# Up-projection of one decoder layer: attention's Strassen units with five doubled products in place of seven single ones

## The chip, the cores and the metric

The kernel runs on one NeuronCore of a Trainium2 chip. The metric is the device time of one execution in microseconds; the median of the runs counts. PE is the matrix engine, PEld its weight loads, DVE the vector engine, ACT the scalar engine, POOL the GpSimd engine, SP the engine that only issues DMAs here. PSUM is the memory that matmuls write to; one of its banks holds 512 float32 for each of the 128 partitions.

## What is computed

One layer of a decoder over 512 tokens of width 2048 in float32. The part that matters here is the merge of the two branches and what stands around it:

```python
merged = jax.nn.sigmoid(g_a) * (y_a @ w_up_a[i]) + jax.nn.sigmoid(g_b) * (y_b @ w_up_b[i])
x = x + merged @ w_o[i]
```

`y_a` (gated spatial mixing) and `y_b` (stick-breaking attention) are 512 x 1024, both `w_up` are 1024 x 2048, and the gates `g_a`, `g_b` are 512 x 2048. Ahead of it stands the combined input projection, behind it the output projection `w_o`, a SwiGLU layer and a gate with per-layer embeddings.

## The kernel before

**Precision.** Each float32 operand is kept as a high part (`hi`, rounded by a copy on ACT) and a low part (`lo`, the rest, by a subtraction on DVE). A product is hi x hi + hi x lo + lo x hi; the first factor is the stationary one (weights), the second the moving one (activations).

**Units.** A unit is a 256 x 256 block of weights against 256 x 512 of activations, as a 2 x 2 matter of blocks. A plain unit ("P") does eight block products (`mm3` with 512 columns in pairs of blocks). A Strassen unit ("S") does seven products of 256 columns, with sums of blocks prepared ahead. `pair` works off all units that make one 256-wide stripe of the output (the index `j`, eight stripes in a stage): it takes the next weights, usually for two units at a time, and calls `Pair.add`. I call such a call with two units a pass. `Pair.add` runs over the seven products (L691) and, within each, over the two units of the pass.

**Single and doubled products.** A single product (L713 to L716) is `mm3`: three matmuls of 256 columns, wh x hi (L297), wh x lo (L298), wl x hi (L299), and products share banks: `a` and `q` take two products each, `z` one, `y` two, so four banks for a stripe. A doubled product (L695 to L705) is two matmuls at L703: wh against hi and lo side by side (512 columns), and wl against hi (256 columns) added into the left half. It fills a bank by itself, and the two halves have to be added afterwards. With five doubled products a stripe has five such banks and the bank `y`, six in all.

**Banks.** `bank()` hands out tiles of the pool `psm`, which has six banks; `small_bank()` has the other two, `psa`, for other use. A tile can only be written when the readers of the tile that had the bank before are through.

**Adding up.** In the last pass of a stripe, a generator puts the seven products together on ACT and DVE, one step behind each product: `mix` (L719) for single products, two ACT copies of 512 columns (L726) and six additions on DVE (L729); `mix_doubled` (L749) for doubled ones, with four ACT copies of 256 columns (L759) and, with five doubled, ten additions on DVE (L762).

**The stage of the up-projection** is the loop from L1383. For each stripe `j` there are: the pair for branch a (`"PPPP"`, two banks, 512-column matmuls), the pair for branch b (`"PPPP"` for `j` = 0, since `until` is 1 there, `"SSSS"` for `j` = 1 to 7), and for `j` = 1 to 5 a small projection `ple_pair` (two banks). Ahead of each pair the gate's stripe is loaded from DRAM (`gsp`, L1385, issued by SP at L526) into the lowest free place of the arena `wholes`. Three ticks later `gate` multiplies it by the row of norms (`scaled`, DVE, L1255) and takes the sigmoid (ACT, L1390). Then the pair's result is multiplied in: a's straight out of its two banks (DVE, L1399, two halves), b's out of the mixed tile (L1396). Last, a's stripe is added to b's (L1403), a's place in the arena is given back, and two ticks later the sum is stored (`mix`, L1377). The next stage, `w_o`, loads these stripes as its activations (`ms`) and splits them (ACT L287, DVE L288).

**Weights.** SP loads them, POOL adds a third block in flight (L371), DVE makes two more sums (L383), ACT the high parts (L367), DVE the low parts (L364). There are three slots of split weights, so those of about two passes stand ready ahead.

**Order.** Each engine works off its instructions in one order, which the framework fixes when the program is built; PE waits at the first matmul whose operand or bank is not ready. In the rows below, b's stripes begin where PE's rows change from 512 to 256 columns.

Of the kernel before, what the change touches and what calls it, by code (L numbers as in the profile page):

```python
# [71 lines left out]
def hybrid_layer(  # L72
# [44 lines left out]
    class Arena:  # L117
# [28 lines left out]
        def give(self, block):  # L146
            self.turns += 1
            self.given[block.start // P : -(-(block.start + block.n) // P)] = self.turns
            holes = sorted(self.holes + [(block.start, block.n)])
            self.holes = holes[:1]  # L150
            for s, n in holes[1:]:
                if sum(self.holes[-1]) == s:
                    self.holes[-1] = (self.holes[-1][0], self.holes[-1][1] + n)
                else:
                    self.holes.append((s, n))
# [48 lines left out]
    def after(n, fn):  # L204
        heapq.heappush(waiting, (clock[0] + n, next(names), fn))
# [318 lines left out]
    def load(src, n=1024, how="old"):  # L524
        b = take(n, how)
        nc.sync.dma_start(out=b.f(0, 1024), in_=src)  # L526
        return b
# [291 lines left out]
    def pair(forms, last=False, j=0, until=None, parts_done=None, at=0,  # L819
             home=lambda: None, doubled=0):  # L820

        until = until or (0,) * len(forms)
        kinds = now("".join(f.kind for f in forms), until, j)
        p = Pair(kinds, home, doubled)
        for k, n in doubles(kinds, at):
            slot, ws = next_weights()
            fs = forms[k : k + n]
            p.add(kinds[k], ws, [f.plain() if j < until[k] else f.get() for f in fs])  # L830
            for f, m in zip(fs, until[k : k + n]):
                if j == m - 1:
                    f.use_plain()
                if last:
                    f.free()
            slots.append(slot)
            if parts_done and k + n == kinds.find("P"):
                last_parts(p, forms[k + n :], parts_done)
                break
        return p  # L840
# [40 lines left out]
    def ple_operands(raw=None):  # L881
        first = raw is not None
        raw = raw or ple_raw(nc.sync)
        ps_p.extend(parts.take(1024, "high") for _ in range(2))
        for k in (0, T):
            ops = split_into(*(x.own(k, k + T) for x in ps_p), raw.f(k, k + T))
            if first:
                in_turn(*ops)
        give(raw)

    def ple_pair(j, weights=None):
        slot, ((wh, wl),) = weights.get() if weights else next_weights()
        if not weights:
            prepare_early()
            prepare_late()
        o = wide()
        banks = bank(), bank()
        for k in range(2):
            xh, xl = (x.own(k * T, (k + 1) * T) for x in ps_p)
            for i, ps in enumerate(banks):  # L900
                s = 2 * i + k
                mm3(ps, wh[:, s], wl[:, s], xh, xl, k == 0, k == 1)
        for i, ps in enumerate(banks):
            nc.scalar.activation(o[:, i * T : (i + 1) * T], ps, AF.Copy)
        d = tc.dram_tile([P, 1024], F32, name=nm("ple"))
        (nc.gpsimd if weights else nc.sync).dma_start(out=d, in_=o)
        ple_spill[j] = d
        slots.append(slot)
        tick()

    def ple_done():
        give(*ps_p)
        ps_p.clear()
# [339 lines left out]
    def scaled(o, row):  # L1253
        b = o.rearrange("p (b t) -> p b t", t=T)
        nc.vector.tensor_tensor(out=b, in0=b, in1=row.unsqueeze(1).to_broadcast([P, 2, T]),  # L1255
                                op=ALU.mult)
# [119 lines left out]
    def store(n, j, block):  # L1376
        nc.sync.dma_start(out=spill[n, j], in_=block.f())  # L1377
        there.add((n, j))
        give(block)
# [3 lines left out]
    for j in range(KU):  # L1383
        for b in "ab":
            s = load(gate_spill[b, j], 1024, "low")  # L1385
            g = s.f()

            def gate(g=g):
                scaled(g, row1)
                nc.scalar.activation(g, g, AF.Sigmoid)  # L1390

            after(3, gate)
            pr = pair([ys[b, i] for i in range(4)], last=j == KU - 1, j=j,
                      until=(b == "b",) * 4)
            if pr.n["S"]:
                nc.vector.tensor_tensor(out=g, in0=g, in1=pr.o, op=ALU.mult)  # L1396
            else:
                for h, ps in zip((g[:, :T], g[:, T:]), pr.ends()):
                    nc.vector.tensor_tensor(out=h, in0=h, in1=ps, op=ALU.mult)  # L1399
            if b == "a":  # L1400
                part[j] = s
            else:
                nc.vector.tensor_tensor(out=g, in0=g, in1=part[j].f(), op=ALU.add)  # L1403
                give(part.pop(j))
                after(2, lambda j=j, s=s: store("mix", j, s))
        if not j:
            ple_operands()
        elif j < 6:
            ple_pair(j + 2)
            if j == 5:  # L1410
                ple_done()
# [51 lines left out]
    for c, units in enumerate(hs):  # L1463
# [3 lines left out]
        for j in range(KU):  # L1467
            if j == KU - 1 and c < len(hs) - 1:
# [4 lines left out]
                      doubled=7)  # L1473
# [144 lines left out]
```

## Time and profile before

| | us |
|---|---|
| median of 3 runs | 2652.05 (2650.84 to 2654.67) |
| profiled execution, its own time | 2647.41 |
| its span, first to last instruction | 2645.7 |
| the stage of the up-projection in it | about 811 to 1004 |

The profile is of one execution. "Busy" is time in which an engine had an instruction under way; a row of the groups gives line, engine, operation, tiles and shapes, the count, then the sum and the mean of one, then the idle time before them. A row of the timeline gives start and duration in us, then engine and line; in square brackets the idle time before it and what ended it. Rows of equal instructions in a row are merged with their count.

### The profile page before, as it was taken

How to read it: one execution, taken by the hardware profiler on the slowest of the kernel's cores; microseconds unless marked ns; L12 is line 12 of the kernel's file. 1: busy time of each engine (PE TensorE's matmuls, PEld its weight loads, DVE VectorE, ACT ScalarE, POOL GpSimd, SP SyncE). 2: the span in 40 equal slices, each digit the busy share in tenths (PEclk: the TensorE clock that was granted, in tenths of full speed). 3: DMA queues.
4: the chain of work that ended last, by engine and by line, in shares of the span. 5: the costliest groups of instructions: out<-in, count | busy, mean ns of one | idle time of the engine just before them, and what ended most of it. 6: DMA issues, size and time to landing. Idle time of an engine off the chain costs nothing.

```text
span 2645.7 us, 43096 instructions
## 1 busy us (share of the span) xinstructions
PE 2631.0 (99%) x15454; PEld 2310.3 (87%) x15454; DVE 2300.3 (87%) x3953; ACT 1431.3 (54%) x2279; POOL 455.7 (17%) x573
## 2 busy tenths in 40 slices
PE   9999999999999999999999999999999999999999
PEld 7888888889998998888888888888888888889888
DVE  8687878787888779999888888888889989989898
ACT  7756565665555445465444444444445445455543
POOL 0222222232220001102111111111110211211010
PEclk9999999999999999999999999999999999999999
DMA  6777777777777879989988888788877989988884
GB/s 207 186 195 172 193 171 187 178 188 191 178 192 243 253 242 285 255 262 239 233 199 206 199 203 205 195 211 198 206 183 225 256 222 271 228 237 262 246 268 136
DMA packets 294533, 569.10 MB, mean 215 GB/s; under 512 B 26800, under 2 KB 137648, under 8 KB 294320
## 3 DMA queue, kind: packets, MB, share of 16 engines
q1 hardware_dynamic: 230240, 444.70, 51.3%
q0 software_dynamic: 63792, 121.14, 28.6%
q8 instruction: 121, 1.98, 0.3%
q14 instruction: 92, 0.75, 0.1%
q10 hardware_dynamic: 288, 0.52, 0.1%
HBM read 514.88 MB, written 51.38 MB: 214 GB/s over the span
## 4 chain that ended last, share of the span: by engine, by line
PE 91%; DVE 5%; DMA 2%; issue 1%; ACT 1%; SPq 0%; POOL 0%; DVEq 0%; ACTq 0%
PE ps L703 57%; PE ps L299 8%; PE ps L298 8%; PE ps L297 8%; PE small L703 6%; DVE wlo L364 1%; DVE parts L288 1%; DVE wholes L535 1%; PE small L1131 1%; PE small L1183 1%; PE small L1057 1%; DMA wholes<-hid 1%; DVE wholes L383 0%; PE small L1242 0%; ACT whi L367 0%
## 5 line engine op out<-in xcount | busy, mean ns | idle before, releaser
L703 PE MATMUL ps<-parts,whi 128*128 128x512 f32 x4390 | 1469.9, 398 | 0.1
L367 ACT ACTIVATE whi<-wholes 128x512 fp32r<-128x512 f32 (+2 forms) x948 | 883.5, 946 | 717.8 <-DVE wholes L383 324.3
L364 DVE TENSOR_TENSOR wlo<-wholes,whi 128x512 fp32r<-128x512 f32 (+2 forms) x948 | 993.3, 1083 | 40.4 <-ACT whi L367 39.9
L703 PEld LDWEIGHTS ps<-parts,wlo 128*128 128x128 f32 x4390 | 823.7, 188 | 188.0 <-DVE wlo L364 3.4
L703 PE MATMUL ps<-parts,wlo 128*128 128x256 f32 x4390 | 869.3, 279 | 1.4 <-DVE wlo L364 1.4
L703 PEld LDWEIGHTS ps<-parts,whi 128*128 128x128 f32 x4390 | 708.0, 189 | 9.5 <-issue 1.9
L299 PE MATMUL ps<-parts,wlo 128*128 128x256 f32 (+1 forms) x1706 | 550.8, 324 | 1.6 <-DVE wlo L364 1.6
L298 PE MATMUL ps<-parts,whi 128*128 128x256 f32 (+1 forms) x1706 | 551.3, 324 | 0.9 <-DVE parts L288 0.9
L297 PE MATMUL ps<-parts,whi 128*128 128x256 f32 (+1 forms) x1696 | 545.0, 323 | 2.6 <-ACT parts L287 1.8
L383 DVE TENSOR_TENSOR wholes<-wholes 128x256 f32<-128x256 f32 x848 | 357.5, 422 | 19.0 <-DMA wholes<-w_up_b 2.3
L298 PEld LDWEIGHTS ps<-parts,whi 128*128 128x128 f32 x1706 | 322.9, 189 | 34.1 <-DVE parts L288 2.7
L762 DVE TENSOR_TENSOR out<-out,ps 128x256 f32<-128x256 f32 x525 | 216.6, 416 | 151.8 <-ACT out L759 151.4
L299 PEld LDWEIGHTS ps<-parts,wlo 128*128 128x128 f32 x1706 | 323.3, 189 | 27.2 <-DVE wlo L364 2.3
L297 PEld LDWEIGHTS ps<-parts,whi 128*128 128x128 f32 x1696 | 320.6, 190 | 28.5 <-ACT parts L287 2.9
L371 POOL DMA_DIRECT2D wholes<-w_ffn_in x169 | 147.6, 873 | 703.5 <-DVE wholes L383 216.0
L371 POOL DMA_DIRECT2D wholes<-w_in x132 | 117.7, 896 | 551.2 <-DMA wholes<-w_in 125.0
L703 PE MATMUL small<-parts,whi 128*128 128x512 f32 x480 | 190.2, 396 | 0.0
L288 DVE TENSOR_TENSOR parts<-wholes,parts 128x1024 fp32r<-128x1024 f32 (+3 forms) x145 | 128.7, 902 | 10.5 <-ACT parts L287 10.5
L287 ACT ACTIVATE parts<-wholes 128x256 fp32r<-128x256 f32 (+3 forms) x145 | 112.0, 796 | 46.4 <-DVE wholes L535 35.0
L759 ACT ACTIVATE out<-ps 128x256 f32<-128x256 f32 x279 | 104.3, 385 | 57.3 <-PE ps L703 53.6
L1441 ACT ACTIVATE out<-out 128x512 f32<-128x512 f32 x44 | 27.9, 633 | 162.4 <-DVE out L1440 162.4
L371 POOL DMA_DIRECT2D wholes<-w_ffn_out x64 | 56.0, 875 | 337.2 <-DVE wlo L364 83.8
(139 smaller groups left out, 1867.0 us busy)
## 6 DMA issues: line engine op xcount, KB each, us to landing
wholes<-w_ffn_in SPq DMA_DIRECT2D x169, 384.0 KB, 5.6
wholes<-w_in SPq DMA_DIRECT2D x132, 384.0 KB, 5.1
wholes<-w_ffn_in SPq DMA_DIRECT2D x169, 256.0 KB, 4.9
wholes<-w_ffn_in POOLq DMA_DIRECT2D x169, 256.0 KB, 5.3
wholes<-w_in SPq DMA_DIRECT2D x132, 256.0 KB, 4.3
wholes<-w_in POOLq DMA_DIRECT2D x132, 256.0 KB, 5.1
wholes<-w_ffn_out SPq DMA_DIRECT2D x64, 384.0 KB, 6.1
wholes<-x SPq DMA_DIRECT2D x46, 512.0 KB, 5.8
```

The costliest lines, as they stand in the source:

```text
L287: return (nc.scalar.activation(hi, src, AF.Copy), nc.vector.tensor_tensor(out=lo, in0=src, in1=hi.bitcast(F32), op=ALU.subtract))
L288: nc.vector.tensor_tensor(out=lo, in0=src, in1=hi.bitcast(F32), op=ALU.subtract))
L297: nc.tensor.matmul(ps, sh, mh, start=start, stop=False)
L298: nc.tensor.matmul(ps, sh, ml, start=False, stop=False)
L299: return nc.tensor.matmul(ps, sl, mh, start=False, stop=stop)
L364: in_turn(nc.vector.tensor_tensor(out=self.lo[:, blocks], in0=r, in1=h.bitcast(F32), op=ALU.subtract))
L367: in_turn(nc.scalar.activation(h, r, AF.Copy))
L371: nc.gpsimd.dma_start(out=raw[:, 3:5], in_=self.src[:, 1:3], accum_op=ALU.add)
L383: in_turn(nc.vector.tensor_tensor(out=o, in0=x, in1=y, op=ALU.add))
L703: m = nc.tensor.matmul(out, l, r, start=first and k == 0, stop=last and k == 1)
L759: in_turn(nc.scalar.activation(out, x, AF.Copy, scale=scale))
L762: in_turn(nc.vector.tensor_tensor(out=out, in0=x, in1=y, op=op))
```

## The change

The pair of the up-projection gets `doubled=5` for branch b (and 0 for a, as before). Nothing else is edited.

```diff
             after(3, gate)
             pr = pair([ys[b, i] for i in range(4)], last=j == KU - 1, j=j,
-                      until=(b == "b",) * 4)
+                      until=(b == "b",) * 4, doubled=5 * (b == "b"))
             if pr.n["S"]:
```

For `j` = 0, where all four units are plain, `doubled` has no effect. For `j` = 1 to 7, `Pair.add` takes the doubled branch for products 0 to 4 and the single one for products 5 and 6 (bank `y`), and `mix_doubled` is used in place of `mix`.

## Prediction

> **What bounds the kernel now.** First the page's busy times: PE is busy for all but 15 us of the span. Then the table by stretch, over the rounds j = 2 to 6 of the up-projection: PE has no idle time at all there, while DVE is idle for 115.77 - 89.13 = 26.6 us. So time changes in this stage only if PE's own work changes or PE is made to wait; DVE's and ACT's work counts where it makes PE wait.
>
> ```profile
> PE 2631.0 (99%) x15454; PEld 2310.3 (87%) x15454; DVE 2300.3 (87%) x3953; ACT 1431.3 (54%) x2279; POOL 455.7 (17%) x573
> ...
> 867.35:983.12 115.77, 115.77 (x709) 104.44 (x708) 89.13 (x123) 53.79 (x65) 8.74 (x10) 1.00 0.83 247
> ```
>
> Then PE's timeline. The first two rows are the same kind of pass in the input projection, with five doubled products already: from its first doubled matmul to its first single one. The other rows are the starts of branch b's seven Strassen stripes, S(1) to S(7), and (at 924.82) the end of the fourth.
>
> ```profile
> 801.08 0.40 PE L703 MATMUL ps<-parts,whi 128*128 128x512 f32 x1
> ...
> 804.59 0.28 PE L297 MATMUL ps<-parts,whi 128*128 128x256 f32 x1
> ...
> 843.64 0.28 PE L297 MATMUL ps<-parts,whi 128*128 128x256 f32 x1
> ...
> 867.35 0.28 PE L297 MATMUL ps<-parts,whi 128*128 128x256 f32 x1
> ...
> 891.04 0.28 PE L297 MATMUL ps<-parts,whi 128*128 128x256 f32 x1
> ...
> 914.75 0.28 PE L297 MATMUL ps<-parts,whi 128*128 128x256 f32 x1
> ...
> 924.82 0.40 PE L297 MATMUL ps<-parts,whi 128*128 128x512 f32 x1
> ...
> 938.45 0.28 PE L297 MATMUL ps<-parts,whi 128*128 128x256 f32 x1
> ...
> 962.14 0.28 PE L297 MATMUL ps<-parts,whi 128*128 128x256 f32 x1
> ...
> 983.12 0.28 PE L297 MATMUL ps<-parts,whi 128*128 128x256 f32 x1
> ```
>
> Since matmuls overlap, the distance of starts is the cost, not the duration. A stripe of 28 single products took 924.82 - 914.75 = 10.07 us, 0.360 us each. Ten doubled products took 804.59 - 801.08 = 3.51 us, 0.351 us each.
>
> **Term 1, PE's own work.** Five products x four units x seven stripes = 140 products go from three matmuls to two, with the same 768 columns: 140 x 0.009 = **1.3 us less**. The trace speaks against more: what counts is columns, nearly.
>
> The Trainium skill says otherwise (TensorE: Matmul & The Clock Gate, "Back-to-back issue gap"): in a sustained stream of weight loads and matmuls a matmul of 512 columns comes every 131 ns and one of 128 every 81 ns. With an unknown 256-column gap x between these, a product would save 3x - (131 + x) = 31 to 131 ns, an estimate of 4 to 18 us for the 140. The rows here (351 ns for 512 and 256 columns) don't agree, so it is no part of the sum.
>
> **Term 2, the banks.** The stripe of b used four of the six banks of `psm`; it will use all six. Two of the six hold a's result of the same round until DVE has multiplied both halves into the gate (L1399). The banks come round in order, so the fifth doubled product needs the one that L1399's first half frees, and the bank `y` the one of its second half. The fifth product begins eight products into the stripe, at S + 8 x 0.351 = S + 2.81, and `y` at S + 3.51. Here is when L1399 ran, per round: the first half in rounds 1, 2, 6 and 7, and the second in 3, 4 and 5, where the second decides.
>
> ```profile
> 848.49 0.69 DVE L1399 TENSOR_TENSOR wholes<-wholes,ps 128x512 f32<-128x512 f32 x1 [0.52 <-ACT wholes L1390]
> ...
> 873.90 0.69 DVE L1399 TENSOR_TENSOR wholes<-wholes,ps 128x512 f32<-128x512 f32 x1 [0.52 <-ACT wholes L1390]
> ...
> 896.58 0.68 DVE L1399 TENSOR_TENSOR wholes<-wholes,ps 128x512 f32<-128x512 f32 x1
> ...
> 919.10 0.68 DVE L1399 TENSOR_TENSOR wholes<-wholes,ps 128x512 f32<-128x512 f32 x1
> ...
> 942.02 0.68 DVE L1399 TENSOR_TENSOR wholes<-wholes,ps 128x512 f32<-128x512 f32 x1
> ...
> 966.50 0.69 DVE L1399 TENSOR_TENSOR wholes<-wholes,ps 128x512 f32<-128x512 f32 x1 [1.13 <-PE ps L298]
> ...
> 987.19 0.69 DVE L1399 TENSOR_TENSOR wholes<-wholes,ps 128x512 f32<-128x512 f32 x1
> ```
>
> End of L1399 less the need, by round: 1: 849.18 - 846.45 = 2.73. 2: 874.59 - 870.16 = 4.43. 3: 897.26 - 894.55 = 2.71. 4: 919.78 - 918.26 = 1.52. 5: 942.70 - 941.96 = 0.74. 6: 967.19 - 964.95 = 2.24. 7: 987.88 - 985.93 = 1.95. Sum **16.3 us**, in which PE stands with all that is queued behind that matmul. Before, this lateness cost nothing: b's four banks were others.
>
> Whether it comes anew each round depends on what L1399 waits for. In round 5:
>
> ```profile
> 926.25 0.68 DVE L729 TENSOR_TENSOR out<-ps,out 128x512 f32<-128x512 f32 x1
> ...
> 928.31 1.22 DVE L1396 TENSOR_TENSOR wholes<-wholes,out 128x1024 f32<-128x1024 f32 x1
> ...
> 931.19 1.22 DVE L1403 TENSOR_TENSOR wholes<-wholes 128x1024 f32<-128x1024 f32 x1
> ...
> 932.43 0.34 SPq L526 DMA_DIRECT2D wholes<-gsp  x1
> ...
> 938.46 1.23 DVE L1255 TENSOR_TENSOR wholes<-wholes 128x1024 f32<-128x1024 f32 x1 [2.03 <-DMA wholes<-gsp]
> ...
> 939.72 1.06 ACT L1390 ACTIVATE wholes<-wholes 128x1024 f32<-128x1024 f32 x1 [4.90 <-DVE wholes L1255]
> ```
>
> b's previous stripe ends on PE at 924.82; DVE subtracts `y`, multiplies by the gate, adds a's part (L1403, until 932.41). That frees the place in the arena for a's next gate, whose load SP issues at 932.43, 0.02 us later. DVE waits for the load, then comes the sigmoid, then L1399. The chain starts from b's previous end, as PE's need does, so a wait in one round moves both and the next round waits again.
>
> **Term 3, DVE and ACT.** Per stripe, five additions of 256 columns and one of 512 become eight and two, and two ACT copies of 512 become four of 256:
>
> ```profile
> L726 ACT ACTIVATE out<-ps 128x512 f32<-128x512 f32 x34 | 19.9, 592 | 15.4 <-PE ps L299 15.4
> ...
> L759 ACT ACTIVATE out<-ps 128x256 f32<-128x256 f32 x279 | 104.3, 385 | 57.3 <-PE ps L703 53.6
> ...
> L762 DVE TENSOR_TENSOR out<-out,ps 128x256 f32<-128x256 f32 x525 | 216.6, 416 | 151.8 <-ACT out L759 151.4
> ...
> L762 DVE TENSOR_TENSOR out<-out,p 128x512 f32<-128x512 f32 x93 | 64.4, 692 | 3.2
> ```
>
> That is 3 x 0.416 + 0.692 = 1.94 us more on DVE and 4 x 0.385 - 2 x 0.592 = 0.36 us more on ACT per stripe, 13.6 and 2.5 us in all; DVE's 26.6 us of idle time covers it. What counts is how late the last subtraction ends. Where five products are doubled already:
>
> ```profile
> 602.20 0.40 PE L703 MATMUL ps<-parts,whi 128*128 128x512 f32 x1
> ...
> 604.48 0.68 DVE L762 TENSOR_TENSOR out<-ps,out 128x512 f32<-128x512 f32 x1
> ```
>
> It ends 605.16 - 602.20 = 2.96 us after PE, against 926.93 - 924.82 = 2.11 now: 0.85 us later. In rounds 2 to 7 this moves the gate's load, and so L1399, by as much: up to 6 x 0.85 = 5.1 us more of waits. Against that, the 2.73 us by which PE stands in round 1 let DVE catch up before round 2, whose L1399 is late because DVE has no pause there, and part of the rest may be covered (first rival). I let these cancel and take 16.3, with 16.3 + 5.1 = 21.4 as the upper end and 0 as the lower.
>
> **Term 4, the end of the stage.** The stripe of j = 7 goes through DRAM to the next stage, and PE waits for it there:
>
> ```profile
> 1001.01 4.63 DMA mix<-wholes
> ...
> 1013.05 0.50 PE L298 MATMUL ps<-parts,whi 128*128 128x512 f32 x1 [0.40 <-DVE parts L288]
> ...
> 1025.26 0.39 PE L297 MATMUL ps<-parts,whi 128*128 128x256 f32 x1 [0.51 <-ACT parts L287]
> ```
>
> No cover here: 0.85 us later on DVE is **0.85 us** more.
>
> **Sum.** 16.3 - 1.3 + 0.85 = 15.9 us on the profiled execution's 2647.41, 2663.3. That execution lies 4.6 us under the median of the runs, so against the median: 2652.05 + 15.9 = **2668**.
>
> **Rivals.**
>
> *First, not slower: the order covers the wait.* The order of matmuls is fixed when the program is built, and it isn't always that of the source:
>
> ```profile
> 958.56 2.09 DVE L364 TENSOR_TENSOR wlo<-wholes,whi 128x1280 fp32r<-128x1280 f32 x2
> ...
> 1044.61 1.07 PE L703 MATMUL ps<-parts,whi 128*128 128x512 f32 x4
> ...
> 1046.18 0.39 PE L703 MATMUL ps<-parts,wlo 128*128 128x256 f32 x1 [0.27 <-DVE wlo L364]
> ```
>
> The source alternates 512, 256, 256, 512; here four of 512 stand together, ahead of the 256 whose low weights were late. If products 0 to 3 of the second pass were put ahead of product 4 of the first, PE would have 8 x 0.351 = 2.81 us of work in front of each wait; their banks are open and the weights there (for round 6 split by 960.65, before 962.14). It decides where it covers 2.81 us: all rounds but the second, 4.43 - 2.81 = 1.6 us left, so 2652.05 + 1.6 - 1.3 + 0.85 = 2653.2. Against it: the order was made before it was known how late the load lands on the chip (DVE's 2.03 us of waiting in round 5), so a wait that was not foreseen has no cover. Chance 0.20.
>
> The Trainium skill (TensorE: Matmul & The Clock Gate, "The mechanism") has matmuls start and end strictly in program order. By that nothing ready passes the waiting one when the program runs, and only a rearranged program can cover; the rising starts of the rows agree.
>
> *Second: the wait comes once.* If the gate's load went by SP's own pace and not by b's end, PE would wait only for the largest lateness: 2652.05 + 4.4 - 1.3 + 0.85 = 2656. Against it stands the 0.02 us between L1403 and the load. Chance 0.07.
>
> *Third: matmuls cost by number.* At 0.120 us each (0.360 / 3), 140 fewer are 16.8 us; without waits 2652.05 - 16.8 + 0.85 = 2636. The rows of doubled products speak against it. Chance 0.03. The skill's gaps, quoted above, would point this way.
>
> That the edit does nothing is hardly possible: seven of eight stripes take the doubled branch.
>
> **From cases to numbers.** The forecast has 0.66, with its own range 2659 to 2674: rounds 1 and 2 covered leave 16.3 - 7.2 = 9.1 us of waits, and all of the 5.1 gives 2652.05 + 21.4 - 1.3 + 0.85 = 2673; a microsecond on each side is for the runs' scatter. More than that 0.04. The measurement can tell about 0.2% (5.3 us). The first and second rival are within it: 0.27. Slower 0.70, faster 0.03. The range has to take in the first rival down to no wait at all (2651.6, less the scatter): 2650.5 to 2674.
>
> **What would show it.** Right: a wait of PE at the fifth product or at `y` of b's first pass in rounds 1 to 7, ended by DVE L1399, 0.7 to 5 us each; doubled products at 0.351 us; the gate's load still right behind L1403; the last subtraction near 3 us behind PE. Wrong: no such waits, with the second pass's first products moved ahead (first rival); one wait and then none (second); or L1399 much earlier against S, since nothing else in the sum is large.

## The result, and the profile after

The changed kernel takes 2664.27 us (median of 6 runs, 2660.46 to 2667.44) against 2652.26 us for the kernel before in the same comparison (6 runs, 2650.61 to 2655.61): 12.0 us more, ratio 1.0047 with a 95% interval of 1.0036 to 1.0057. The profiled execution took 2661.96 us, its span is 2660.0 us.

From the page of the kernel after: the busy times, the chain of work that ended last by engine, and the group of the doubled matmuls (after the second bar its idle time and what ended it). Below them stand the chain and the group of the kernel before.

```profile
PE 2630.8 (99%) x15314; PEld 2300.9 (87%) x15314; DVE 2310.9 (87%) x3981; ACT 1432.0 (54%) x2293; POOL 469.1 (18%) x573
...
PE 80%; DVE 8%; DMA 7%; issue 3%; ACT 2%; SPq 0%; POOL 0%; DVEq 0%; ACTq 0%; POOLq 0%
...
L703 PE MATMUL ps<-parts,whi 128*128 128x512 f32 x4530 | 1517.9, 398 | 11.5 <-DVE wholes L1399 10.8
```

```profile
PE 91%; DVE 5%; DMA 2%; issue 1%; ACT 1%; SPq 0%; POOL 0%; DVEq 0%; ACTq 0%
...
L703 PE MATMUL ps<-parts,whi 128*128 128x512 f32 x4390 | 1469.9, 398 | 0.1
```

PE has 140 matmuls fewer, its busy time is the same to 0.2 us, and the span is 14.3 us longer. So the work is the same and PE stands idle. The group had 0.1 us of idle time before it and has 11.5 now, and it names who it waits for: 10.8 of these end with L1399, the multiplication of a's result out of its two banks. The stretch of rounds j = 2 to 6, from S(2) to S(7), was 115.77 us long before, with PE busy throughout. After:

```profile
869.36:992.90 123.54, 116.04 (x610) 98.75 (x608) 96.56 (x141) 55.51 (x75) 8.72 (x10) 1.00 0.77 229
```

It is 7.8 us longer, and 7.5 us of it PE is idle (123.54 - 116.04). The granted clock, third from the end, is 1.00: nothing here comes from the clock. PE's timeline has the waits one by one, in brackets, with the start of one stripe (919.96) to measure from:

```profile
849.80 0.50 PE L703 MATMUL ps<-parts,whi 128*128 128x512 f32 x1 [1.33 <-DVE wholes L1399]
...
855.62 0.50 PE L297 MATMUL ps<-parts,whi 128*128 128x512 f32 x1 [0.82 <-DVE out L762]
...
876.72 0.50 PE L703 MATMUL ps<-parts,whi 128*128 128x512 f32 x1 [1.63 <-DVE wholes L1399]
...
900.79 0.50 PE L703 MATMUL ps<-parts,whi 128*128 128x512 f32 x1 [1.46 <-DVE wholes L1399]
...
919.96 0.39 PE L703 MATMUL ps<-parts,whi 128*128 128x512 f32 x1
...
924.88 0.49 PE L703 MATMUL ps<-parts,whi 128*128 128x512 f32 x1 [1.74 <-DVE wholes L1399]
...
949.78 0.50 PE L703 MATMUL ps<-parts,whi 128*128 128x512 f32 x1 [1.39 <-DVE wholes L1399]
...
975.06 0.50 PE L703 MATMUL ps<-parts,whi 128*128 128x512 f32 x1 [1.29 <-DVE wholes L1399]
...
1000.12 0.50 PE L703 MATMUL ps<-parts,whi 128*128 128x512 f32 x1 [1.96 <-DVE wholes L1399]
```

One wait on L1399 per round, seven in all, each at the fifth product. The line at 855.62 is new and was not foreseen: in round 1 the small projection behind b's stripe waits for a bank that DVE's adding up (L762) still reads. Here is the chain that leads to the wait at 924.88, round 4, from DVE's timeline and then SP's:

```profile
914.52 1.22 DVE L1403 TENSOR_TENSOR wholes<-wholes 128x1024 f32<-128x1024 f32 x1
...
921.78 1.23 DVE L1255 TENSOR_TENSOR wholes<-wholes 128x1024 f32<-128x1024 f32 x1 [2.52 <-DMA wholes<-gsp]
...
924.13 1.28 DVE L1399 TENSOR_TENSOR wholes<-wholes,ps 128x512 f32<-128x512 f32 x2 [0.52 <-ACT wholes L1390]
```

```profile
915.77 0.33 SPq L526 DMA_DIRECT2D wholes<-gsp  x1
```

L1403 of the round before ends at 915.74, the load of a's next gate is issued 0.03 us later, DVE idles 2.52 us for it, and L1399's first half ends about 924.82 (two halves of some 0.69 us in the row); PE starts again at 924.88.

At the end of the stage the last stripe is stored at 1015.31, 10.36 us behind the end of b's last stripe on PE (1004.95), where it was 7.81 us (1001.01 - 993.20). The waits of the next stage were 1.18 us before (0.40, 0.51 and 0.27, shown ahead) and are 2.30 now, in two:

```profile
1038.85 0.62 PE L297 MATMUL ps<-parts,whi 128*128 128x256 f32 x3 [1.39 <-ACT parts L287]
...
1059.77 0.50 PE L703 MATMUL ps<-parts,wlo 128*128 128x256 f32 x2 [0.91 <-DVE wlo L364]
```

By round, from the timelines of PE and DVE. S(j) is the start of b's stripe in round j, E(j) its end, where the next row of PE starts. A doubled stripe of b without any wait lasts 9.86 us (experiments 1 and 2); "lost" is what it lasts beyond that. "Late" is the end of L1399's first half less S + 2.81, the need (in the forecast's rounds 3 to 5 the second half less S + 3.51). "Moved" is what the order put ahead of the fifth product: b's matmuls there beyond the 16 that stand there in the order of the source, at 0.351 us for two.

| round | late, forecast | late, after | moved | stripe of b | lost |
|---|---|---|---|---|---|
| 1 | 2.73 | 3.74 | 13 = 2.3 us | 12.42 | 2.56 (0.82 of it at 855.62) |
| 2 | 4.43 | 4.50 | 16 = 2.8 us | 11.74 | 1.88 |
| 3 | 2.71 | 3.16 | 9 = 1.6 us | 11.56 | 1.70 |
| 4 | 1.52 | 2.05 | 1 = 0.2 us | 11.85 | 1.99 |
| 5 | 0.74 | 1.48 | 0 | 11.52 | 1.66 |
| 6 | 2.24 | 1.61 | 1 = 0.2 us | 11.40 | 1.54 |
| 7 | 1.95 | 4.37 | 13 = 2.3 us | 12.05 | 2.19 |
| sum | 16.3 | 20.9 | 9.3 us | 82.5 (before 70.5) | 13.5 |

### The profile page after: what moved, and what is told of

Same layout as the page of the kernel before. It is cut to its first block, busy times and chain, and to the rows that moved or that the text cites. A ratio compares the mean times of both kernels' runs of the same rounds, so it can differ in the third digit from the quotient of the medians.

```text
span 2660.0 us, 42856 instructions
## 1 busy us (share of the span) xinstructions
PE 2630.8 (99%) x15314; PEld 2300.9 (87%) x15314; DVE 2310.9 (87%) x3981; ACT 1432.0 (54%) x2293; POOL 469.1 (18%) x573
## 3 DMA queue, kind: packets, MB, share of 16 engines
q8 instruction: 120, 1.97, 0.3%
## 4 chain that ended last, share of the span: by engine, by line
PE 80%; DVE 8%; DMA 7%; issue 3%; ACT 2%; SPq 0%; POOL 0%; DVEq 0%; ACTq 0%; POOLq 0%
PE ps L703 55%; PE small L703 6%; PE ps L299 5%; PE ps L297 5%; PE ps L298 5%; DVE wlo L364 2%; DMA wholes<-gsp 1%; DVE out L762 1%; DMA wholes<-w_ffn_out 1%; DVE wholes L535 1%; DVE parts L288 1%; DMA wholes<-hid 1%; DMA wholes<-w_up_b 1%; PE small L1183 1%; PE small L1131 1%
## 5 line engine op out<-in xcount | busy, mean ns | idle before, releaser
L703 PE MATMUL ps<-parts,whi 128*128 128x512 f32 x4530 | 1517.9, 398 | 11.5 <-DVE wholes L1399 10.8
L364 DVE TENSOR_TENSOR wlo<-wholes,whi 128x512 fp32r<-128x512 f32 (+2 forms) x948 | 994.4, 1085 | 40.6 <-ACT whi L367 40.2
L703 PEld LDWEIGHTS ps<-parts,wlo 128*128 128x128 f32 x4530 | 849.7, 188 | 193.6 <-DVE wlo L364 3.8
L703 PE MATMUL ps<-parts,wlo 128*128 128x256 f32 x4530 | 896.9, 279 | 1.9 <-DVE wlo L364 1.9
L703 PEld LDWEIGHTS ps<-parts,whi 128*128 128x128 f32 x4530 | 730.5, 189 | 24.9 <-DVE wholes L1399 13.6
L299 PE MATMUL ps<-parts,wlo 128*128 128x256 f32 (+1 forms) x1566 | 510.4, 327 | 1.9 <-DVE wlo L364 1.9
L298 PE MATMUL ps<-parts,whi 128*128 128x256 f32 (+1 forms) x1566 | 510.6, 327 | 0.6 <-DVE parts L288 0.5
L297 PE MATMUL ps<-parts,whi 128*128 128x256 f32 (+1 forms) x1556 | 503.5, 327 | 4.3 <-ACT parts L287 2.9
L762 DVE TENSOR_TENSOR out<-out,ps 128x256 f32<-128x256 f32 x560 | 231.5, 417 | 168.9 <-ACT out L759 168.6
L298 PEld LDWEIGHTS ps<-parts,whi 128*128 128x128 f32 x1566 | 295.6, 189 | 33.8 <-DVE parts L288 2.6
L297 PEld LDWEIGHTS ps<-parts,whi 128*128 128x128 f32 x1556 | 292.8, 189 | 30.6 <-ACT parts L287 4.5
L703 PE MATMUL small<-parts,whi 128*128 128x512 f32 x480 | 190.1, 396 | 0.0
L759 ACT ACTIVATE out<-ps 128x256 f32<-128x256 f32 x300 | 110.5, 382 | 60.2 <-PE ps L703 56.5
L288 DVE TENSOR_TENSOR parts<-wholes,parts 128x1024 fp32r<-128x1024 f32 (+3 forms) x145 | 129.1, 906 | 9.1 <-ACT parts L287 9.0
```

The lines of the kernel that those rows point to most:

```text
L288: nc.vector.tensor_tensor(out=lo, in0=src, in1=hi.bitcast(F32), op=ALU.subtract))
L297: nc.tensor.matmul(ps, sh, mh, start=start, stop=False)
L298: nc.tensor.matmul(ps, sh, ml, start=False, stop=False)
L299: return nc.tensor.matmul(ps, sl, mh, start=False, stop=stop)
L364: in_turn(nc.vector.tensor_tensor(out=self.lo[:, blocks], in0=r, in1=h.bitcast(F32), op=ALU.subtract))
L703: m = nc.tensor.matmul(out, l, r, start=first and k == 0, stop=last and k == 1)
```

## Experiments

Theory: b's stripe now needs the two banks that a's unread result holds, and L1399 sets when they come free. Rivals: doubling by itself costs the time (a longer sum on DVE, another order on PE); or the late load of the gate does, with the banks only passing it on; or the order of the matmuls, rearranged around the wait, does.

**1. a's result in other banks.** Branch a takes its two banks from `psa`, which no matmul of this stage uses otherwise; five products stay doubled.

```diff
-                self.banks[name] = small_bank() if name == small else bank()
+                self.banks[name] = small_bank() if name == small or self.aside else bank()
...
-                      until=(b == "b",) * 4, doubled=5 * (b == "b"))
+                      until=(b == "b",) * 4, doubled=5 * (b == "b"), aside=b == "a")
```

> Branch a's two result banks come from the pool psa, whose two banks have no other use in this stage; b keeps its five doubled products and all six banks of psm. Theory (PE waits because a's result still holds two of the six banks): no wait of PE on L1399 is left, the products of the first and second pass stand in the order of the source again, and what stays is 1.3 us less work of PE and about 1 us at the end of the stage: 2651 to 2654 us, within 0.2% of before. Rival (the added additions on DVE and the copies on ACT are what costs): 2660 to 2665 us, as after.

Measured: 2653.10 us (11 runs; before 2653.07), ratio 1.0000 (0.9991 to 1.0008). The waits of PE from 800 to 1120 us, by the line waited for (us in total, times, longest):

```profile
PE ps L297 <- DVE out L762: 2.0, 1, 2.0
PE ps L297 <- ACT parts L287: 2.0, 1, 2.0
PE ps L703 <- DVE wlo L364: 0.4, 1, 0.4
PE ps L298 <- DVE parts L288: 0.2, 1, 0.2
```

No wait on L1399 is left, although L1399 itself is as late as ever: its first half ends 6.50, 6.77, 5.16, 4.08, 4.45, 6.78 and 7.51 us behind S. Late is not the same as waited for; the bank makes it so. The 12 us are gone, six of seven stripes last 9.86 us, and no product is moved any more. That leaves 0.21 us gained per stripe (10.07 before), 1.5 us in seven, which doesn't appear in the time: in this profile round 1 has the wait on L762 again, now of 2.05 us, and the end of the stage waits 2.6 us in place of 1.2.

**2. a's gate loaded early.** The banks stay as in the change; the gate's place (a's, and b's too) is the arena's oldest free place instead of its lowest.

```diff
-            s = load(gate_spill[b, j], 1024, "low")
+            s = load(gate_spill[b, j], 1024, "old")
```

> The changed kernel, but the gate's stripe is loaded into the place of the arena that has been free longest, not the lowest one. Theory (L1399 is late because the gate's load waits for the place that L1403 frees): the load goes out several us before L1403, L1399 ends earlier by as much, and the waits go in the rounds where DVE had to wait for the load (3 to 7): 2652 to 2658 us. Rival (the load is held back by SP's queue, or DVE is late anyway): load and waits stay, 2661 to 2667 us.

Measured: 2654.44 us (10 runs), ratio 1.0007 (0.9998 to 1.0016). DVE's timeline in round 4:

```profile
909.69 1.22 DVE L1403 TENSOR_TENSOR wholes<-wholes 128x1024 f32<-128x1024 f32 x1
...
914.35 1.22 DVE L1255 TENSOR_TENSOR wholes<-wholes 128x1024 f32<-128x1024 f32 x1
...
917.47 1.28 DVE L1399 TENSOR_TENSOR wholes<-wholes,ps 128x512 f32<-128x512 f32 x2 [0.26 <-ACT wholes L1390]
```

L1255 has no wait for the load any more. L1399's first half ends 2.33 us behind S (915.83), ahead of the need at 2.81; in rounds 1, 2 and 7 it is 4.03, 4.33 and 4.09, and there moved products cover the rest. No wait on L1399 appears, stripes last 9.86 us (round 1: 10.18, round 6: 9.92), and from S(1) to E(7) it is 148.45 us against 149.56 before. So either half of the cause removes the cost: the bank, or the lateness of its reader. The 1.1 us are given back again: 2.9 us of waits behind the stage (1.2 before), and another at 1185 us, of which experiment 5 tells.

**3. The order of the source.** The changed kernel, with b's matmuls chained in the order in which the source issues them: each doubled matmul, and the last of the three of a single product, calls the function below. No engine waits for these links; they only keep the order from being rearranged.

```diff
+    def in_order(m):
+        if before_it:
+            tc.add_manual_dep(
+                m.ins, before_it[-1],
+                mybir.DependencyInfo(mybir.DependencyClass.NoSync,
+                                     mybir.DependencyReason.DATA),
+                reason="in its place among the products")
+        before_it.append(m.ins.name)
...
```

> The changed kernel with b's matmuls tied to the order of the source, so that no product of the second pass stands ahead of the fifth product of the first. Theory (the rearranged order covers part of the lateness of L1399, 20.9 us in sum over the seven rounds against 12.7 us that PE loses): about 8 us more, 2669 to 2676 us, with waits of 1.5 to 4.5 us. Rival (the rearrangement gains nothing, since L1399 comes later by what it moves ahead): 2661 to 2667 us.

Measured: 2666.93 us (4 runs; before 2653.07), ratio 1.0055 (1.0041 to 1.0069). That misses my theory's 2669 to 2676 us and lies within the rival's range. Against the kernel before of its own comparison it is 13.9 us, where the change was 12.0; the medians of the two differ by 2.7 us, and the intervals of the two ratios overlap. So by the medians the order is worth some 2 to 3 us, not clear of the noise, and not the full price of the cover that is gone. The waits view from 800 to 1120 us (the added lines shift L703 and L1399 to L714 and L1415), and two stretches of the table by windows, behind the waits of rounds 1 and 7, whose third number from the end is the granted clock:

```profile
PE ps L714 <- DVE wholes L1415: 13.7, 7, 4.0
```

```profile
853.00:855.00 2.00, 2.00 (x10) 1.90 (x9) 0.30 (x1) 1.40 (x2) 0.00 (x0) 0.50 1.00 301
...
1003.00:1005.00 2.00, 2.00 (x9) 1.81 (x9) 0.13 (x1) 0.00 (x0) 0.00 (x0) 0.50 0.84 215
```

The waits are 3.32, 1.43, 1.22, 1.30, 1.07, 1.34 and 4.00 us; the stripes last 14.96, 11.55, 11.35, 11.42, 11.20, 11.46 and 15.53 us. In rounds 2 to 6 this order loses 7.7 us beyond 9.86 a stripe, less than the rearranged one (8.8). Only rounds 1 and 7 got something from being rearranged: 4.8 lost there after the change, 10.8 here, of which some 2.9 are not waits but the half clock behind them (14.96 - 9.86 - 3.32 and 15.53 - 9.86 - 4.00, less 0.27 each with which PE starts again, as in rounds 2 to 6: 11.55 - 9.86 - 1.43 is 0.26). The reason is in DVE's timeline: L1403 ends 7.31 us behind b's end in round 1 and 8.7 in rounds 2 to 5 here, but 10.61, 10.58, 9.41, 8.70 and 8.70 after the change (in round 1 some 1.5 us of the difference is the half clock, which delays b's end here). There PE's products run ahead of the waiting one, DVE's sums of that stripe come behind L1399 anyway, and so b's result is finished later relative to PE; the next load and the next L1399 are later by that. So cover in one round was paid back in the next, as far as two profiles can show it.

**4. Six banks without doubling.** The kernel before, with the second products of `a` and `q` in banks of their own: single products, and six banks per stripe. ACT copies each half of `a` and `q` by itself (four copies in place of two).

```diff
-                        ps = self.at(name)[:, 256 * h : 256 * h + 256]
-                        ends = not (self.both and name in "yz") and (h == 1 or name == "z")
+                        own = self.apart and name in "aq"
+                        ps = (self.at((name, h))[:, :256] if own else
+                              self.at(name)[:, 256 * h : 256 * h + 256])
+                        ends = own or (not (self.both and name in "yz")
+                                       and (h == 1 or name == "z"))
...
```

> The kernel before, seven single products, but the two products that share the bank a and the two that share q get a bank each (left half), and ACT copies each half by itself: six banks for a stripe of b with the matmuls and DVE's additions of before. Theory (the count of banks is the cause, not the doubling): PE waits on L1399 in the same place, 16.3 us by the rows of before, less up to 9 us that the order may cover: 2658 to 2668 us. Rival (the doubled products and the additions they need are the cause): 2651 to 2654 us, no wait on L1399.

Measured: 2663.30 us (4 runs), ratio 1.0042 (1.0026 to 1.0057). The waits view (its L1408 is L1399) and two windows in round 2:

```profile
PE ps L297 <- DVE wholes L1408: 7.0, 7, 2.1
```

```profile
874.00:876.00 2.00, 1.83 (x8) 1.83 (x9) 0.71 (x2) 0.00 (x0) 0.41 (x1) 0.55 0.92 261
876.00:878.00 2.00, 2.00 (x13) 2.00 (x12) 0.00 (x0) 1.02 (x1) 0.46 (x1) 0.60 0.93 248
```

No product is doubled and DVE's sums are the old ones, yet there are seven waits on the same line, and the loss is 10.2 us, where the change lost 12.0. That settles it between the theory and the first rival: the number of banks costs the time. The doubling's longer sum makes the waits longer (10.8 us after the change, 7.0 here), but only through the banks, as experiment 1 shows. That the two losses are so near is in part chance: in rounds 2 and 7 (waits of 2.04 and 2.06 us) the clock falls behind them, and the stripe of round 2 lasts 13.87 us, 10.07 + 2.04 + 0.27 and 1.5 us more.

**5. The early load alone.** The edit of experiment 2 made to the kernel before.

> The kernel before (seven single products), with the gate's stripe loaded into the place that has been free longest: the control of e2. Theory (the earlier load only matters where PE waits on L1399, which it doesn't before): the load goes out several us earlier, PE's stretch from the first Strassen stripe to the end of the last stays near 149.6 us, time within 0.1% of before. Rival (the earlier load helps or harms by itself): 4 us or more off before.

Measured: 2655.69 us (12 runs; before 2652.48 of 29), ratio 1.0017 (1.0006 to 1.0028): the early load by itself costs some 3 us, which I had not expected (my theory was within 0.1% of before). PE's timeline, at the end of the stage and in the stage after that:

```profile
1016.35 0.73 PE L297 MATMUL ps<-parts,whi 128*128 128x512 f32 x2 [2.38 <-ACT parts L287]
...
1184.98 0.74 PE L297 MATMUL ps<-parts,whi 128*128 128x256 f32 x4 [2.35 <-ACT parts L287]
```

SP's timeline shows where the first begins, in the kernel before and then here:

```profile
1001.01 0.33 SPq L1377 DMA_DIRECT2D mix<-wholes  x1
1002.15 0.33 SPq L340 DMA_DIRECT2D wholes<-w_o  x1
1002.53 0.99 SPq L526 DMA_DIRECT2D wholes<-mix  x1
```

```profile
1002.74 0.33 SPq L340 DMA_DIRECT2D wholes<-w_o  x1
1004.21 0.33 SPq L526 DMA_DIRECT2D wholes<-xT  x1
1006.56 0.80 SPq L526 DMA_DIRECT2D wholes<-mix  x2
```

The next stage's activations were issued 0.38 us behind a weight load; now a load of `xT` stands between, and they go out at 1006.56. Taking another place for one tile changes which places are free for every later load; that this put the load of `xT` ahead is my reading and not tested. The wait near 1185 us is in the profiles of all four kernels with this edit (2.84, 2.35, 2.65 and 1.80 us) and in no other. Behind it the granted clock is 0.50 for 3.41 us in experiments 2, 5 and 7, which costs more beside the wait; in experiment 6 it stays at 1.00. Why the wait arises there was not followed further.

**6. Both remedies.** Experiments 1 and 2 together.

> Both cures together: a's result in psa and the early load, b with five doubled products. Theory: no wait on L1399 and none of the small projection on the mix of round 1 (2.0 us in e1); PE's stretch 1.3 to 1.5 us under before's 149.6, and at the end of the stage PE waits 1 to 2 us more than before: 2650 to 2654 us, same as before. Rival (something else in the doubled path costs): over 2656 us.

Measured: 2654.58 us (12 runs), ratio 1.0012 (1.0003 to 1.0021), 0.6 us above the range that I had expected. In the stage this is the best of all: every stripe lasts 9.86 us, and S(1) to E(7) takes 148.10 us, 1.5 less than before. The early load's waits elsewhere (2.9 us behind the stage, 2.65 at 1185) take more than that.

**7. The last round single.** Experiment 2, with the stripe of round 7 single again, against the waits at the end of the stage.

```diff
-                      until=(b == "b",) * 4, doubled=5 * (b == "b"))
+                      until=(b == "b",) * 4, doubled=5 * (b == "b" and j < KU - 1))
```

> e2 (five doubled, early load) with the last stripe, j = 7, left at seven single products. Theory (term 4: the later end of the doubled mix on DVE lengthens the waits at the end of the stage): PE's waits behind the last stripe, 2.8 us in e2 against 1.2 before, go back to about 1.2 to 1.8, time 2651.5 to 2653.5. Rival (these waits have another cause, such as the order of the loads): they stay at 2.5 us or more.

Measured: 2656.14 us (12 runs), ratio 1.0016 (1.0005 to 1.0026). A miss: the waits behind the stage shrink to 1.7 us, but the one at 1185 us stays (1.8), and a new one of 0.6 us on L1399 comes. The time is that of experiment 5, the early load alone.

**8. Other banks, rounds 2 to 6 only.** Experiment 1, with the stripes of rounds 1 and 7 single.

> A's result in the two banks of psa, and five products doubled in the rounds j = 2 to 6 only; round 1 and round 7 stay single as in the kernel before. My theory: doubling by itself is worth 0.21 us a stripe (10.07 to 9.86 us), and what the run with the psa banks in all seven rounds lost again came from the ends: DVE's mix in round 1 (the wait on L762 of 2.05 us) and the late store of the last stripe (waits behind the stage). Then no wait of PE in rounds 1 to 7, five stripes of 9.86 us and two of 10.07, waits behind the stage near 1.2 us as before, and 2651.4 us, ratio 0.9995 to 0.9998: at the edge of what can be measured. Rival: the time is given back wherever PE runs earlier, since the loads for the next stage set its start; then the waits behind the stage grow by about the 1 us gained and the ratio is 1.0000.

Measured: 2651.14 us (11 runs; before 2651.62 of 15), ratio 0.9998 (0.9989 to 1.0007). The time fits my theory and can't be told from no change; the profile fits the rival. No wait is left in rounds 1 to 7, five stripes last 9.86 us. But behind the stage:

```profile
PE ps L297 <- ACT parts L287: 2.6, 1, 2.6
PE ps L298 <- DVE parts L288: 1.1, 2, 0.8
PE ps L703 <- DVE wlo L364: 0.3, 1, 0.3
```

That is 4.0 us in place of 1.2, and the last stripe's store goes out at 1001.36, where it was 1001.01. PE is there earlier and the transfers are not. No version was faster than the kernel before by as much as can be measured.

## Why the prediction came out as it did

**What bounds the kernel:** right. PE was without a pause in the stage, and every us of the change is a us in which it waits.

**Term 1** (1.3 us less): right. A doubled stripe without waits lasts 9.86 us in place of 10.07, 1.5 us in seven. The third rival, a cost by number of matmuls, is out: at 0.120 us each, 20 matmuls fewer would make a stripe 2.4 us shorter, and it is 0.21 shorter. The gaps that the Trainium skill gives (TensorE: Matmul & The Clock Gate, "Back-to-back issue gap") are out with it: by them a stripe would be an estimated 0.6 us shorter at least (20 products by 31 ns).

**Term 2** (16.3 us): the mechanism was right in each link: the bank, the line, the fifth product, each round anew, the load 0.03 us behind L1403. Experiments 1 and 4 show it from both sides: without the shared banks the cost is gone, with them alone and no doubling it is there. Only in rounds 3 to 7 does DVE wait for that load, though; in rounds 1 and 2 L1255 follows without a pause, and L1399 is late because DVE is. The size is 12.7 us (13.5 lost less the 0.82 at 855.62). Two errors stand against each other in it. L1399 is later than taken from the kernel before: the sum of lateness is 20.9 us, not 16.3. And the order covers part, 9.3 us of matmuls put ahead of the waits: 20.9 - 9.3 = 11.6, and PE takes some 0.16 us more per wait from the bank's release to its full pace. That these two nearly cancel, and the forecast came near, is in part luck.

**The first rival** (the order covers the wait) therefore happened in four of seven rounds, with less effect than it promised. I had given cover 2.81 us per round, as if nothing followed from it. Experiment 3 shows the net worth: some 2 to 3 us of the whole time, not clear of the noise, and 4.9 us in the stripes of the two profiles, from the first and last rounds alone, of which 2.9 is the half clock that shorter waits avoid. The argument against it, that the order doesn't know how late the load lands, fits rounds 4 to 6, where one matmul at most was moved; this was not tried by itself. That nothing passes a waiting matmul when the program runs is not shown by the rising starts which I named, since a timeline is sorted by them. Experiment 3 agrees with it better: PE stood 3.32 us at the fifth product, with products behind it that ran ahead of it after the change. **The second rival** (one wait only) is out: seven waits.

**Term 3** (0.85 us per round, cancelled against DVE's catching up and the cover): the size is near. b's sum is added (L1403) 8.70 us behind PE in rounds 4 and 5 in place of 7.59, 1.1 us more; the cancelling was a guess. The last subtraction ends 3.2 us behind PE there, forecast 2.96. The raw lateness of 20.9 us is close to the 21.4 which I had as the upper end with nothing cancelled. But in the order of the source (experiment 3), where nothing is covered, it is 14.3 us by the same measure (3.40, 1.52, 1.30, 1.38, 1.16, 1.42 and 4.09): there DVE does catch up while PE stands, by more than term 3 adds. Where PE works on instead of waiting, DVE catches up less. So catching up and cover are largely the same microseconds, which I had taken for two. Here lies the mis-sized term: the forecast of 15.9 us is 3.9 us above the 12.0 by which the medians differ and 1.6 above the 14.3 of the two profiles; term 2 with its cover is 3.6 us too high, and part of that is made up by what was not foreseen.

**Term 4** (0.85 us): 1.1 us (2.30 - 1.18), though for a store that is 2.55 us later (10.36 - 7.81); most of that was covered, against my "no cover here". The store is later by more than the forecast 0.85 because the last subtraction is: it ends 5.78 us behind b's end on PE (1010.73 - 1004.95), where it was 3.25 (996.45 - 993.20). Six of the sums and an L364 come behind PE's end now, where two sums did; L1255 and L288 stand among them in both kernels.

**Not foreseen:** the 0.82 us at 855.62. Six banks per stripe, kept until a longer adding up has read them, also meet the next user of the pool.

In the profiles: -1.5 + 12.7 + 0.8 + 1.1 = 13.1 of the 14.3 us by which the spans differ; the rest lies outside this stage, in no one place. The medians differ by 12.0. The profiled execution of the kernel before lies 4.9 us below the median (2647.41 against 2652.26), that of the change 2.3 below. Which waits the other executions of before have can't be seen; so the small waits behind the stage, 1 to 3 us in experiments 1, 2, 6, 7 and 8, are shown for one execution each, and that they are what gives the gain back is likely and not shown.

## What to carry to other kernels

Before an operation is given more banks, list who holds the others at that moment and when the last reader of each is through: a reader that was late at no cost becomes the bound as soon as its bank is next in turn. Moving the unread result to a pool that is idle there removed the cost (ratio 1.0000), and so did hurrying its reader (1.0007, which can't be told apart from it); but the load moved earlier came with new waits in two later stages. And work that is put ahead of a wait may buy little where what ends the next wait starts from that work's end, as experiment 3 suggests.

## What the runs showed of the hardware

**The clock can fall after a wait of PE of about two microseconds.** Behind waits of 3.32 and 4.00 us (experiment 3) and of 2.04 and 2.06 us (experiment 4) the granted clock is 0.50 for 3.41 us, which costs 1.4 to 1.5 us beside the wait. (A row of 2 us that such a stretch covers in part shows a value in between, such as 0.55.) In experiment 1 the same comes behind 1.97 us of wait, at the end of the stage:

```profile
1018.00:1020.00 2.00, 1.98 (x12) 1.69 (x12) 2.00 (x3) 0.00 (x0) 0.87 (x1) 0.91 0.97 327
1020.00:1022.00 2.00, 2.00 (x7) 1.71 (x7) 1.44 (x3) 0.46 (x1) 0.00 (x0) 0.50 0.80 210
1022.00:1024.00 2.00, 2.00 (x8) 1.52 (x8) 0.69 (x1) 0.62 (x2) 0.45 (x1) 0.74 0.98 291
```

The shortest waits with a fall behind them are 1.79 us (at 2495.28) and 1.80 us, both in experiment 7. The second, from PE's timeline and the table by windows:

```profile
1181.66 0.74 PE L297 MATMUL ps<-parts,whi 128*128 128x256 f32 x4 [1.80 <-ACT parts L287]
```

```profile
1182.00:1184.00 2.00, 2.00 (x14) 2.00 (x13) 2.00 (x2) 1.04 (x2) 0.87 (x1) 0.65 0.16 54
1184.00:1186.00 2.00, 2.00 (x12) 2.00 (x11) 0.00 (x1) 0.00 (x0) 0.00 (x0) 0.50 0.94 251
```

Behind the 2.05 us at 856.83 in experiment 1, the 2.38 at 1016.35 in experiment 5, the 2.65 at 1184.93 in experiment 6 and the 2.64 at 1028.11 in experiment 8 it stays at 1.00, as it does behind all waits of the change, up to 1.96 us. So from about 1.8 us on it can go either way, and the length of the wait alone doesn't decide.

What may decide is where a wait lies. The half clock begins at 874.20 and 997.08 in experiment 4, at 852.14 and 1002.32 in experiment 3, at 1182.61 and 2496.74 in experiment 7: 122.88, 150.18 and 1314.13 us apart, which is 36, 44 and 385 times 3.4133 us. This fits a clock that is set anew at fixed intervals of 3.41 us, as long as the half clock lasts. The 1.80 us of experiment 7 (1179.86 to 1181.66) lie wholly within one interval (1179.20 to 1182.61). Counted back 48 intervals from the fall at 1019.64, a border in experiment 1 lies at 855.80, and it cuts the 2.05 us there (854.78 to 856.83) in half. Where the limit lies is not shown: in experiment 2, with a border at 1015.47 counted back 50 intervals from the fall at 1186.14, a wait from 1013.67 to 1015.54 has 1.80 us in one interval, and the clock stayed at 1.00.

The Trainium skill (TensorE: Matmul & The Clock Gate, "Why this matters for your kernels") asks for no pauses of PE above some 3 us; the falls behind 1.79 to 2.06 us here differ from that. It also says ("What's actually happening") that the window in which activity is counted runs freely, which agrees with like waits ending differently. Seven waits of 2 us could thus have cost more than their sum. Of the change's seven only the last, 1.96 us, is longer than the shortest with a fall behind it; that the clock stayed there is luck, and the change's other executions are not shown.
